# Two stacked transformer blocks in fp32 on one core: the "up" products of five feed-forward stages are turned, so that weight tiles are held in TensorE and the rows of both token tiles move

## The chip, the cores and the metric

The kernel runs on one core of one Trainium2 chip. The metric is the time of one execution in microseconds (us), as the device counts it. Engines are named as in the profile: PE is TensorE (matrix products), DVE is VectorE, ACT is ScalarE, POOL is GpSimd, SP issues most of the transfers.

## The reference, cut to what matters

256 rows (two token tiles of 128) with 1024 columns go through four layers. The first two layers each have a gated feed-forward part, a mixing part of four attention and convolution branches, and a second gated feed-forward part. The last two layers each have an attention part with gates and a plain feed-forward part.

```python
def _swiglu(x, w_in, w_out):                      # 1024 -> 2 x 2816 -> 1024
    gate, up = jnp.split(x @ w_in, 2, axis=-1)
    return (jax.nn.silu(gate) * up) @ w_out

hn = _modulate(_rms_norm(h, norm_g[l, 2]), sh3, sc3)
h = h + 0.5 * g3[:, None, :] * _swiglu(hn, ffn2_w_in[l], ffn2_w_out[l])

h = rmsnorm(x, norm_mlp)                          # 1024 -> 4096 -> 1024
return x + jnp.square(jax.nn.relu(h @ w_up)) @ w_down
```

All inputs are fp32, and so is the result.

## The kernel before, in words

**Stages.** The program is one straight list of instructions for each engine. Ten stages follow each other: 0 feed-forward, 1 mixing, 2 feed-forward, 3 feed-forward, 4 mixing, 5 feed-forward (layers one and two), then 6 attention, 7 feed-forward (called `mlp`), 8 attention, 9 `mlp` (layers three and four). A feed-forward stage has an up phase (`gemm_in`) and an out phase (`gemm_out`).

**Products in three parts.** An fp32 operand is split into `hi` (rounded to the type fp32r) and `lo`, the rest: ScalarE casts `hi`, VectorE subtracts to get `lo`. A product is then three fp32r products that add up in one PSUM bank: hi·hi, hi·lo and lo·hi. Weights come from memory in chunks of 512 KB (`fetch`, issued by SP), and `pump` converts each chunk into `hi` and `lo` on ScalarE and VectorE. `chunk()` hands them to the products in order. Tiles come from an arena of 40 buffers of 4 KB in each partition (`c` in the names of the profile).

**The up phase.** `gemm_in` goes over blocks of 512 output columns (11 in a gated part: 256 gate and 256 up columns; 8 in an `mlp`). For each block it goes over the two token tiles `tt`, and for each of these over eight slices `k` of 128 inputs. The 128x128 slice of the normed, transposed rows (`xT`) is held in the array and 512 columns of weights move:

```python
pe.matmul(ps[:, :n], xh, hi[:, k2], start=k == 0, stop=False)
pe.matmul(ps[:, :n], xh, lo[:, k2], start=False, stop=False)
pe.matmul(ps[:, :n], xl, hi[:, k2], start=False, stop=k == KT - 1)
```

The bank then holds rows by columns. `evac` reads it: in a gated part ScalarE takes the silu of the gate half, VectorE multiplies by the up half; in an `mlp` ScalarE takes the relu, scaled by the rows' norm `n_.rs[tt]`, and VectorE squares it. The result (tile `ev`, 4 buffers) is needed the other way round, with the hidden columns on partitions. So `turn`, a background task, transposes it on TensorE in pieces of 128x128 into another bank, from which ScalarE and VectorE split it into `hi` and `lo`. A gated block has two pieces for each `tt`, an `mlp` block four.

**The out phase.** `gemm_out` holds slices of the hidden rows and moves 512 columns of weights, three products each, in four banks; `residual_gated` and `residual_plain` add the result to `h`.

**What sets the order.** `Plan` keeps a modelled clock for each engine while the program is recorded. Background tasks (`bg`) are recorded between products when their modelled due time has come; `pump` converts chunks ahead while the modelled VectorE and ScalarE are not late. The order is then fixed; on the chip each engine goes through its own list and waits for semaphores. Stages 0, 2, 3 and 5 also stream modulation weights (`ada_w`) between the chunks: `ada_unit` does one VectorE instruction of 1024 columns for each (`CUSTOM_DVE_ANT_0` or `SCALAR_TENSOR_TENSOR c<-c,cond,c`). Nearly all instructions are recorded through one helper, line 183, so the profile is read by tiles and shapes.

Of the kernel before, what the change touches and what calls it, by code (L numbers as in the profile page):

```python
# [70 lines left out]
class Plan:  # L71
# [10 lines left out]
    @staticmethod  # L82
    def box(ap):

        pitch = ap.ap[0][0]
        p, a = divmod(ap.offset, pitch)
        return p, p + ap.ap[0][1], a, a + 1 + sum(s * (n - 1) for s, n in ap.ap[1:])

    @staticmethod
    def meet(a, b):  # L90
        return a[0] < b[1] and b[0] < a[1] and a[2] < b[3] and b[2] < a[3]
# [5 lines left out]
    def put(self, table, ap, stamp):  # L97

        box = self.box(ap)
        kept = [e for e in table.get(ap.name, ()) if not (box[0] <= e[0][0] and e[0][1] <= box[1] and box[2] <= e[0][2] and e[0][3] <= box[3]  # L100
                                                         and (table is self.written or e[1][1] == stamp[1]))]
        table[ap.name] = kept + [(box, stamp)]
# [140 lines left out]
def two_blocks(ctx: ExitStack, tc, w, out, dbg=None, stages=99):  # L243
# [14 lines left out]
    arena = Ring(pool, "c4", NARENA)  # L258
    evr = Ring(pool, "ev", 4)
# [337 lines left out]
    class Normed:  # L597
# [40 lines left out]
        def chain(self, tt):  # L638
# [10 lines left out]
            yield from until(lambda: room(3 if self.keep else 2))  # L649
            self.xT[tt] = arena.take([P, KT, P], R), arena.take([P, KT, P], R)  # L650
            if self.keep:
                self.x[tt] = arena.take([P, KT, P])
# [13 lines left out]
        def free(self):  # L666
            arena.put(6 if self.keep else 4)
# [123 lines left out]
    def gemm_in(n_, blocks, evac):  # L791

        whole, nb = range(4), len(blocks)
        if st["want"] == 0:
            order = [(b, tt, whole[c:c + 1]) for c in whole for b in range(EARLY) for tt in range(2)]
            order += [(b, tt, whole) for b in range(EARLY, nb) for tt in range(2)]
            mine["quota"] = 8
        else:
            order = [(b, tt, whole) for b in range(nb) for tt in range(2)]
# [4 lines left out]
        for b, tt, part in order:  # L804
            n = width(blocks[b])
            if part[0] == 0:
                wait(lambda: psr.has(1), "bank")
                acc[b, tt] = psr.take([P, 512])
                mine["held"] += 1
            ps = acc[b, tt]  # L810
            for ci in part:
# [4 lines left out]
                for k2 in range(2):  # L816
                    k = 2 * ci + k2
                    n_.finish(tt, k)
                    if lo is None:
                        pe.matmul(ps[:, :n], n_.x[tt][:, k], hi[:, k2], start=k == 0, stop=k == KT - 1)  # L820
                    else:
                        xh, xl = n_.xT[tt][0][:, k], n_.xT[tt][1][:, k]
# [989 lines left out]
```

## Time and profile before

| what | value |
|---|---|
| median of 3 runs | 1907.07 us (1906.06 to 1907.81) |
| profiled execution, its own time | 1907.24 us |
| span in its trace (first to last instruction) | 1905.5 us |
| TensorE busy, matrix products | 1864.3 us (98%) |
| TensorE weight loads (beside the products) | 1487.9 us (78%) |
| VectorE busy | 1303.6 us (68%) |
| ScalarE busy | 972.5 us (51%) |
| granted TensorE clock, mean | 0.996 |
| memory read | 394.69 MB, 208 GB/s over the span |

From the writes to `h` in the trace, the stages end near 217, 338, 527, 715, 832, 1018, 1275, 1459, 1716 and 1905 us. The up phases of the stages that the change touches are 338 to 463 (stage 2), 527 to 652 (3), 832 to 957 (5), 1275 to 1370 (7) and 1716 to 1811 (9). A busy share is an average: a busy TensorE is not one at its peak, and the spacing of its products says more.

### The profile page before, as it was taken

How to read it: one execution, taken by the hardware profiler on the slowest of the kernel's cores; microseconds unless marked ns; L12 is line 12 of the kernel's file. 1: busy time of each engine (PE TensorE's matmuls, PEld its weight loads, DVE VectorE, ACT ScalarE, POOL GpSimd, SP SyncE). 2: the span in 40 equal slices, each digit the busy share in tenths (PEclk: the TensorE clock that was granted, in tenths of full speed). 3: DMA queues.
4: the chain of work that ended last, by engine and by line, in shares of the span. 5: the costliest groups of instructions: out<-in, count | busy, mean ns of one | idle time of the engine just before them, and what ended most of it. 6: DMA issues, size and time to landing. Idle time of an engine off the chain costs nothing.

```text
span 1905.5 us, 23848 instructions
## 1 busy us (share of the span) xinstructions
PE 1864.3 (98%) x8672; PEld 1487.9 (78%) x8672; DVE 1303.6 (68%) x2044; ACT 972.5 (51%) x1506; POOL 17.0 (1%) x56
## 2 busy tenths in 40 slices
PE   6999999999999999999999999999999999999998
PEld 5788864888888886668888787888888787888886
DVE  7999796878697967865566646676654546666561
ACT  5544545444454545654445646555543645645460
POOL 0000000000000000000000000000000000000000
PEclk9999999999999999999999999999999999999999
DMA  9989752678688865435565343655574343654460
GB/s 384 382 329 394 259 192 78 234 268 297 246 296 288 334 240 194 156 130 189 192 239 188 111 155 102 215 170 167 180 250 141 125 159 107 197 195 160 146 220 34
DMA packets 110579, 397.32 MB, mean 209 GB/s; under 512 B 12278, under 2 KB 12406, under 8 KB 110460
## 3 DMA queue, kind: packets, MB, share of 16 engines
q1 hardware_dynamic: 109020, 391.88, 59.4%
q10 hardware_dynamic: 1440, 3.91, 0.6%
q8 instruction: 68, 1.11, 0.2%
q14 instruction: 51, 0.42, 0.1%
HBM read 394.69 MB, written 1.05 MB: 208 GB/s over the span
## 4 chain that ended last, share of the span: by engine, by line
PE 87%; DVE 5%; ACT 5%; issue 1%; DMA 1%; POOL 0%; ACTq 0%; POOLq 0%; DVEq 0%
PE bank L183 87%; DVE c L183 3%; ACT sm L183 2%; ACT c L183 2%; DVE sm L183 1%; ACT L175 1%; DMA cond_row<-in_c_dram 0%; DVE ev L183 0%; DMA c<-in_ada_w_dram 0%; DMA c<-in_w_out_b_dram 0%; DVE st L183 0%; DVE h L183 0%; ACT ev L183 0%; ACT junk L183 0%; ACT dl L183 0%
## 5 line engine op out<-in xcount | busy, mean ns | idle before, releaser
L183 PE MATMUL bank<-c,c 128*128 128x512 f32 (+3 forms) x7392 | 1761.9, 396 | 10.9 <-ACT c L183 7.8
L183 PEld LDWEIGHTS bank<-c,c 128*128 128x128 f32 (+1 forms) x7392 | 1350.0, 188 | 327.4 <-issue 45.8
L183 DVE TENSOR_TENSOR c<-c,c 128x1024 fp32r<-128x1024 f32 (+4 forms) x614 | 711.5, 1182 | 233.4 <-ACT c L183 225.4
L183 ACT CAST c<-c 128x1024 fp32r<-128x1024 f32 (+4 forms) x600 | 592.0, 1025 | 112.7 <-PE bank L183 74.7
L183 ACT ACTIVATE ev<-bank 128x256 f32<-128x256 f32 (+1 forms) x100 | 40.0, 401 | 198.4 <-PE bank L183 196.2
L183 DVE CUSTOM_DVE_ANT_0 c<-c,cond_row,col 128x1024 f32<-128x1024 f32 x96 | 121.9, 1275 | 0.0
L183 ACT CAST c<-bank 128x512 fp32r<-128x512 f32 (+1 forms) x100 | 55.2, 553 | 86.5 <-PE bank L183 86.5
L183 DVE TENSOR_TENSOR c<-bank,c 128x512 fp32r<-128x512 f32 (+2 forms) x108 | 69.6, 647 | 24.1 <-ACT c L183 24.1
L183 DVE TENSOR_TENSOR ev<-ev,bank 128x256 f32<-128x256 f32 x88 | 36.4, 417 | 67.4 <-ACT ev L183 67.1
L183 ACT ACTIVATE ev<-bank,st 128x512 f32<-128x512 f32 x56 | 38.5, 688 | 77.6 <-PE bank L183 77.6
L183 ACT ACTIVATE junk<-h 128x512 f32<-128x512 f32 x44 | 27.8, 631 | 95.2 <-DVE h L183 94.8
L183 PEld LDWEIGHTS bank<-con,ev 128*128 128x128 f32 x432 | 55.9, 140 | 25.5 <-issue 4.9
L183 PE MATMUL bank<-con,ev 128*128 128x128 f32 x432 | 72.3, 273 | 3.2 <-DVE ev L183 3.2
L183 ACT CAST c<-ev 128x512 fp32r<-128x512 f32 x28 | 17.4, 620 | 91.4 <-DVE ev L183 91.2
L183 ACT ACTIVATE c<-bank,st 128x512 f32<-128x512 f32 x36 | 24.8, 688 | 75.2 <-PE bank L183 69.7
L183 DVE SCALAR_TENSOR_TENSOR c<-c,cond,c 128x1024 f32<-128x1024 f32 x42 | 53.7, 1278 | 0.0
L183 DVE TENSOR_TENSOR ev<-ev 128x512 f32<-128x512 f32 x32 | 22.1, 690 | 45.5 <-ACT ev L183 45.5
L183 DVE TENSOR_TENSOR ev<-bank,c 128x512 f32<-128x512 f32 x40 | 27.4, 685 | 34.4 <-PE bank L183 34.3
L183 DVE SCALAR_TENSOR_TENSOR c<-c,col,c 128x256 f32<-128x256 f32 x120 | 48.8, 474 | 0.0
L183 ACT ACTIVATE sm<-sm,st 128x128 f32<-128x128 f32 x72 | 31.8, 443 | 17.3 <-DVE st L183 17.3
L183 DVE TENSOR_TENSOR h<-h,bank 128x512 f32<-128x512 f32 x16 | 10.9, 682 | 42.1 <-PE bank L183 42.1
L183 DVE TENSOR_TENSOR c<-ev,c 128x512 fp32r<-128x512 f32 x28 | 19.4, 692 | 23.1 <-ACT c L183 23.0
(106 smaller groups left out, 676.0 us busy)
## 6 DMA issues: line engine op xcount, KB each, us to landing
c<-in_ffn_w_in_dram SPq DMA_DIRECT2D x176, 512.0 KB, 4.8
c<-in_w_in_dram SPq DMA_DIRECT2D x152, 512.0 KB, 4.2
c<-in_ada_w_dram SPq DMA_DIRECT2D x144, 512.0 KB, 5.9
c<-in_ffn_w_out_dram SPq DMA_DIRECT2D x88, 512.0 KB, 5.5
c<-in_w_up_dram SPq DMA_DIRECT2D x64, 512.0 KB, 4.2
c<-in_w_down_dram SPq DMA_DIRECT2D x64, 512.0 KB, 4.3
c<-in_w_out_dram SPq DMA_DIRECT2D x16, 512.0 KB, 4.4
c<-in_w_o_dram SPq DMA_DIRECT2D x16, 512.0 KB, 4.2
```

What stands on the lines that cost most here:

```text
L175: self.eng.preload_act_table_set(table)
L183: return fn(*args, **kw)
```

## The change

In the up phases of stages 2, 3, 5, 7 and 9 the blocks from the third on (`b >= ALONE`, 2) are turned. A 128x128 slice of the weights is held, and the rows of both token tiles move. For this the split rows of every norm lie in one fixed tile `X` of 128 x (8 slices, 4, 128): for each slice `k` hi of tile 0, hi of tile 1, lo of tile 0, lo of tile 1. One product of weight `hi` with all four (512 columns) and one of weight `lo` with the two hi parts (256 columns) replace the three. The bank then has hidden columns on partitions: its first half collects hi·hi and lo·hi, its second half the rows' lo part, and the halves are added afterwards. Nothing has to be transposed. A block is done in two passes (`pairs[tt]`) of two banks each: in a gated part a pass has 128 gate and the 128 matching up columns.

Since tokens now lie along the columns, the `mlp` can't scale by row before the relu; the square of the norm factor (`r2`) is applied in the residual instead, for all blocks of the `mlp`. The arena goes from 40 to 36 buffers, and a norm no longer takes 4 of them. The planner's bookkeeping (`box`, `meet`, `within`) is refined to follow parts of `X`; it records no instructions.

```diff
-    NRAW, NBASE, NMOST, NARENA, SPARE = 8, 18, 16, 40, 6
+    NRAW, NBASE, NMOST, NARENA, SPARE = 8, 18, 16, 36, 6
+    ALONE = 2
+    X = pool.tile([P, KT, 4, P], R, name="X")
...
-            yield from until(lambda: room(3 if self.keep else 2))
-            self.xT[tt] = arena.take([P, KT, P], R), arena.take([P, KT, P], R)
+            self.xT[tt] = X[:, :, tt], X[:, :, 2 + tt]
...
-            order = [(b, tt, whole) for b in range(nb) for tt in range(2)]
+            order = [(b, tt, whole, bool(pairs) and b >= ALONE) for b in range(nb) for tt in range(2)]
...
-                wait(lambda: psr.has(1), "bank")
-                acc[b, tt] = psr.take([P, 512])
-                mine["held"] += 1
+                wait(lambda: psr.has(1 + both), "bank")
+                acc[b, tt] = tuple(psr.take([P, 2, S]) for _ in range(2)) if both else psr.take([P, 512])
+                mine["held"] += 1 + both
...
+                    if both:
+                        n_.finish(0, k)
+                        n_.finish(1, k)
+                        for i, j in enumerate(pairs[tt]):
+                            a = slice(P * j, P * j + P)
+                            pe.matmul(ps[i], hi[:, k2, a], X[:, k], start=k == 0, stop=False)
+                            pe.matmul(ps[i][:, 0], lo[:, k2, a], X[:, k, 0:2], start=False, stop=k == KT - 1)
...
+        def parts(b, x):
+            yield from until(lambda: hid.room(2 * b))
+            hi, lo = hid.at(2 * b)
+            a = slice(2 * (b % 2), 2 * (b % 2) + 2)
+            split(x, hi[:, a], lo[:, a])
+            evr.put()
+
+        def turned(b, g, ps):
+            wait(lambda: evr.has(2 - g), "ev")
+            if g == 0:
+                made[b] = evr.take([P, 2, S])
+            s, x = evr.take([P, S]), made[b]
+            sc_.copy(s, ps[0][:, 1])
+            sc_.copy(x[:, g], ps[1][:, 1])
+            ve.tensor_tensor(s, s, ps[0][:, 0], op=OP.add)
+            ve.tensor_tensor(x[:, g], x[:, g], ps[1][:, 0], op=OP.add)
+            sc_.activation(s, s, AF.Silu)
+            done_bank(2)
+            ve.tensor_tensor(x[:, g], x[:, g], s, op=OP.mult)
+            evr.put()
+            if g == 1:
+                hid.pend.setdefault(2 * b, []).append(bg.add(parts(b, x), urgent=True, due=plan.ready(x)))
...
-        gemm_in(n_, FFN_BLOCKS, evac)
+        gemm_in(n_, FFN_BLOCKS, evac, () if n_.first else ((0, 2), (1, 3)), turned)
...
-            sc_.activation(x, ps, AF.Relu, scale=n_.rs[tt])
+            sc_.activation(x, ps, AF.Relu)
...
+        def turned(b, g, ps):
+            wait(lambda: evr.has(1), "ev")
+            x = evr.take([P, 2, S])
+            for i in range(2):
+                sc_.copy(x[:, i], ps[i][:, 1])
+            for i in range(2):
+                ve.tensor_tensor(x[:, i], x[:, i], ps[i][:, 0], op=OP.add)
+            done_bank(2)
+            sc_.activation(x, x, AF.Relu)
+            ve.tensor_tensor(x, x, x, op=OP.mult)
+            hid.pend.setdefault(4 * b, []).append(bg.add(parts(b, g, x), urgent=True, due=plan.ready(x)))
...
+            if hf == 0:
+                ve.tensor_tensor(r2[:, tt:tt + 1], n_.rs[tt], n_.rs[tt], op=OP.mult)
+            ve.scalar_tensor_tensor(hs, ps, r2[:, tt:tt + 1], hs, op0=OP.mult, op1=OP.add)
...
-        gemm_in(n_, UP_BLOCKS, evac)
+        gemm_in(n_, UP_BLOCKS, evac, ((0, 1), (2, 3)), turned)
```

On TensorE, in the up phase of stage 5 before, two slices `k` of one token tile stand like this (the names are output bank, moving weight tile, held row tile), with two transposes of an earlier result among them:

```order
L183 MATMUL bank273_7762<-c41060_7589,c41016_7243 128x512
L183 MATMUL bank273_7762<-c41061_7590,c41016_7243 128x512
L183 MATMUL bank273_7762<-c41060_7589,c41017_7244 128x512
L183 MATMUL bank272_7719<-con_67,ev210_7759 128x128 x2
L183 MATMUL bank273_7762<-c41065_7645,c41016_7243 128x512
L183 MATMUL bank273_7762<-c41066_7646,c41016_7243 128x512
L183 MATMUL bank273_7762<-c41065_7645,c41017_7244 128x512
```

The same engine in the same phase after, two slices `k` of one pass (the names are output bank, moving `X`, held weight tile):

```order
L191 MATMUL bank300_8319<-X_63,c41054_8130 128x512
L191 MATMUL bank300_8319<-X_63,c41055_8131 128x256
L191 MATMUL bank301_8320<-X_63,c41054_8130 128x512
L191 MATMUL bank301_8320<-X_63,c41055_8131 128x256
L191 MATMUL bank300_8319<-X_63,c41057_8144 128x512
L191 MATMUL bank300_8319<-X_63,c41058_8145 128x256
```

A slice `k` of a whole block was 6 products of 512 columns; it is 4 of 512 and 4 of 256, and the transposes are gone from the turned blocks. Over the program the transposes from `ev` go from 432 to 228, and 1248 products of 256 columns are new.

On VectorE, in the up phase of stage 3 before, the work from one split into a hidden tile to the next split into it (`c<-bank,c` 128x512 is the split of the transposed bank, `c<-c,c` 128x1024 the conversion of a chunk, `SCALAR_TENSOR_TENSOR` a modulation unit):

```order
L183 TENSOR_TENSOR c4780_5344<-bank175_5264,c4779_5343 128x512
L183 TENSOR_TENSOR ev152_5354<-ev151_5353,bank176_5316 128x256
L183 TENSOR_TENSOR c4782_5377<-c4763_5226,c4781_5376 128x1024
L183 SCALAR_TENSOR_TENSOR c4758_5199<-c4766_5274,cond_72,c4758_5199 128x1024
L183 TENSOR_TENSOR c4786_5392<-c4767_5277,c4785_5391 128x1024
L183 SCALAR_TENSOR_TENSOR c4758_5199<-c4770_5289,cond_72,c4758_5199 128x1024
L183 TENSOR_TENSOR ev154_5404<-ev153_5403,bank177_5357 128x256
L183 TENSOR_TENSOR c4790_5412<-c4771_5292,c4789_5411 128x1024
L183 SCALAR_TENSOR_TENSOR c4758_5199<-c4774_5304,cond_72,c4758_5199 128x1024
L183 TENSOR_TENSOR c4780_5344<-bank178_5364,c4779_5343 128x512
```

VectorE after, at the same place, a split and the two passes of the block that follows it:

```order
L191 TENSOR_TENSOR c4764_5620<-ev137_5627,c4763_5619 128x512
L191 TENSOR_TENSOR ev141_5740<-ev141_5740,bank194_5685 128x256
L191 TENSOR_TENSOR ev140_5739<-ev140_5739,bank195_5686 128x256
L191 TENSOR_TENSOR ev140_5739<-ev140_5739,ev141_5740 128x256
L191 TENSOR_TENSOR c4778_5762<-c4759_5611,c4777_5761 128x1024
L191 SCALAR_TENSOR_TENSOR c4742_5473<-c4762_5617,cond_73,c4742_5473 128x1024
L191 TENSOR_TENSOR c4742_5473<-c4742_5473,c4743_5474 1x1024
L191 TENSOR_TENSOR c4782_5788<-c4767_5661,c4781_5787 128x1024
L191 TENSOR_TENSOR ev142_5797<-ev142_5797,bank196_5747 128x256
L191 TENSOR_TENSOR ev140_5739<-ev140_5739,bank197_5748 128x256
L191 TENSOR_TENSOR ev140_5739<-ev140_5739,ev142_5797 128x256
L191 TENSOR_TENSOR c4785_5819<-c4768_5664,c4784_5818 128x1024
```

Where one multiplication stood for each token tile, each pass now has two additions and a multiplication of 256 columns in the same list as the chunk conversions; the split of the hidden tile reads `ev` and not a bank.

## Rows read from the trace of the kernel before

**Rows 1.** The page: busy time by engine, and the chain that ended last.
```profile
PE 1864.3 (98%) x8672; PEld 1487.9 (78%) x8672; DVE 1303.6 (68%) x2044; ACT 972.5 (51%) x1506; POOL 17.0 (1%) x56
...
PE 87%; DVE 5%; ACT 5%; issue 1%; DMA 1%; POOL 0%; ACTq 0%; POOLq 0%; DVEq 0%
```

**Rows 2.** Windows, up phases of stages 2, 3, 5, 7: stretch, length, busy.
```profile
core 0: us, PE busy (x) PEld busy (x) DVE busy (x) ACT busy (x) POOL busy (x), PEclk, DMA share, GB/s
338.00:463.00 125.00, 125.00 (x573) 102.23 (x572) 96.65 (x126) 59.41 (x87) 0.74 (x2) 1.00 0.76 263
527.00:652.00 125.00, 125.00 (x573) 102.45 (x573) 105.96 (x139) 60.18 (x88) 0.74 (x2) 1.00 0.84 295
832.00:957.00 125.00, 125.00 (x574) 102.23 (x573) 75.03 (x89) 58.45 (x85) 0.74 (x2) 1.00 0.58 195
1275.00:1370.00 95.00, 95.00 (x450) 78.33 (x449) 60.00 (x66) 50.47 (x67) 0.74 (x2) 1.00 0.48 150
```

**Rows 3.** Timeline of PE, up phase of stage 5: start, length, group.
```profile
870.00 0.38 PE L183 MATMUL bank<-con,ev 128*128 128x128 f32 x2
870.14 5.74 PE L183 MATMUL bank<-c,c 128*128 128x512 f32 x24
...
955.67 0.38 PE L183 MATMUL bank<-con,ev 128*128 128x128 f32 x2
```

**Rows 4.** Timeline of PE, up phase of stage 7.
```profile
1323.15 0.60 PE L183 MATMUL bank<-con,ev 128*128 128x128 f32 x4
1323.50 5.74 PE L183 MATMUL bank<-c,c 128*128 128x512 f32 x24
...
1358.75 0.60 PE L183 MATMUL bank<-con,ev 128*128 128x128 f32 x4
```

**Rows 5.** Tile bank on PE, out phase of stage 7 (1380 to 1440): first and last start.
```profile
L183 PE MATMUL bank<-c,c x266: 389/389/389, 1379.7 to 1439.8; 128*128 128x512 f32 x133
```

**Rows 6.** Groups by form, PE, 231 to 235: products of 260 columns (stage 1).
```profile
L183 PE MATMUL bank<-c,c 128*128 128x260 f32 x24 | 3.0, 281 | 0.0
```

**Rows 7.** Groups by form, weight loads (PEld), 231 to 235 and 1380 to 1440.
```profile
L183 PEld LDWEIGHTS bank<-c,c 128*128 128x128 f32 x29 | 3.9, 188 | 0.2
...
L183 PEld LDWEIGHTS bank<-c,c 128*128 128x128 f32 x265 | 49.7, 188 | 10.3
```

**Rows 8.** Groups by form, DVE, 527 to 652 (up phase of stage 3).
```profile
L183 DVE TENSOR_TENSOR c<-c,c 128x1024 fp32r<-128x1024 f32 x44 | 53.2, 1218 | 5.3 <-ACT c L183 4.8 <-DMA c<-in_ada_w_dram 0.5
L183 DVE CUSTOM_DVE_ANT_0 c<-c,cond_row,col 128x1024 f32<-128x1024 f32 x22 | 28.1, 1276 | 0.0
L183 DVE SCALAR_TENSOR_TENSOR c<-c,cond,c 128x1024 f32<-128x1024 f32 x7 | 8.9, 1278 | 0.0
L183 DVE TENSOR_TENSOR ev<-ev,bank 128x256 f32<-128x256 f32 x21 | 8.7, 416 | 10.4 <-ACT ev L183 10.4
L183 DVE TENSOR_TENSOR c<-bank,c 128x512 fp32r<-128x512 f32 x10 | 6.8, 684 | 0.7 <-ACT c L183 0.7
L183 DVE TENSOR_TENSOR c<-ev,c 128x512 fp32r<-128x512 f32 x2 | 1.4, 687 | 0.7 <-ACT c L183 0.7
```

**Rows 9.** Groups by form, DVE, 338 to 463 (up phase of stage 2).
```profile
L183 DVE TENSOR_TENSOR c<-c,c 128x1024 fp32r<-128x1024 f32 x41 | 49.7, 1221 | 7.5 <-ACT c L183 6.9 <-DMA c<-in_ffn_w_in_dram 0.5
...
L183 DVE TENSOR_TENSOR ev<-ev,bank 128x256 f32<-128x256 f32 x22 | 9.2, 418 | 16.3 <-ACT ev L183 16.3
```

**Rows 10.** Groups by form, ACT, 527 to 652.
```profile
L183 ACT ACTIVATE ev<-bank 128x256 f32<-128x256 f32 x22 | 8.4, 383 | 47.2 <-PE bank L183 47.2
L183 ACT CAST c<-bank 128x512 fp32r<-128x512 f32 x10 | 5.9, 587 | 13.4 <-PE bank L183 13.4
...
L183 ACT CAST c<-ev 128x512 fp32r<-128x512 f32 x2 | 1.2, 620 | 2.3 <-DVE ev L183 2.3
```

**Rows 11.** Groups by form, DVE, then ACT, 1275 to 1370 (up phase of stage 7).
```profile
L183 DVE TENSOR_TENSOR ev<-ev 128x512 f32<-128x512 f32 x16 | 11.0, 690 | 22.8 <-ACT ev L183 22.8
L183 DVE TENSOR_TENSOR c<-bank,c 128x512 fp32r<-128x512 f32 x15 | 10.4, 690 | 3.5 <-ACT c L183 3.5
...
L183 ACT ACTIVATE ev<-bank,st 128x512 f32<-128x512 f32 x16 | 11.0, 690 | 29.2 <-PE bank L183 29.2
```

More of the change, by code (lines that the diff above doesn't have):

```diff
@@ L99, in put @@
         box = self.box(ap)
-        kept = [e for e in table.get(ap.name, ()) if not (box[0] <= e[0][0] and e[0][1] <= box[1] and box[2] <= e[0][2] and e[0][3] <= box[3]
-                                                         and (table is self.written or e[1][1] == stamp[1]))]
+        kept = [e for e in table.get(ap.name, ()) if not (self.within(e[0], box) and (table is self.written or e[1][1] == stamp[1]))]
         table[ap.name] = kept + [(box, stamp)]
@@ L666, in free @@
         def free(self):
-            arena.put(6 if self.keep else 4)
+            arena.put(2 if self.keep else 0)
     class Final(Normed):
@@ L788, in rows_ready, with gemm_in @@
             upcoming.pop(0)
-    def gemm_in(n_, blocks, evac):
+    def gemm_in(n_, blocks, evac, pairs=(), turned=None):
         whole, nb = range(4), len(blocks)
         if st["want"] == 0:
-            order = [(b, tt, whole[c:c + 1]) for c in whole for b in range(EARLY) for tt in range(2)]
-            order += [(b, tt, whole) for b in range(EARLY, nb) for tt in range(2)]
+            order = [(b, tt, whole[c:c + 1], False) for c in whole for b in range(EARLY) for tt in range(2)]
+            order += [(b, tt, whole, False) for b in range(EARLY, nb) for tt in range(2)]
             mine["quota"] = 8
         else:
-            order = [(b, tt, whole) for b in range(nb) for tt in range(2)]
+            order = [(b, tt, whole, bool(pairs) and b >= ALONE) for b in range(nb) for tt in range(2)]
             if not n_.there[1] or n_.there[1][-1] < KT:
@@ L803, in gemm_in @@
         held, acc = {}, {}
-        for b, tt, part in order:
+        for b, tt, part, both in order:
             n = width(blocks[b])
             if part[0] == 0:
-                wait(lambda: psr.has(1), "bank")
-                acc[b, tt] = psr.take([P, 512])
-                mine["held"] += 1
+                wait(lambda: psr.has(1 + both), "bank")
+                acc[b, tt] = tuple(psr.take([P, 2, S]) for _ in range(2)) if both else psr.take([P, 512])
+                mine["held"] += 1 + both
             ps = acc[b, tt]
@@ L831, in gemm_in, with done_bank @@
             if part[-1] == 3:
[L832 to L833 removed]
+                drain([n_.e[0], n_.e[1]] if both else [n_.e[tt]])
+                (turned if both else evac)(b, tt, acc.pop((b, tt)))
                 mine["quota"] = 3
[L836 to L838 removed]
+    def done_bank(n=1):
+        psr.put(n)
+        mine["held"] -= n
     def gemm_out(nk, lhs, evac, skew, used=lambda k: None):
```

46 lines of the change are left out of this document (31 added, 15 removed).

## The prediction

> **What bounds the kernel now.** I read the busy times first, then the chain, then the stretches that change. TensorE is busy for 98% of the span and makes up 87% of the chain that ended last [rows 1]. In the up phases of stages 2, 3, 5 and 7, TensorE is busy without a break, at a granted clock of 1.00 [rows 2]; stage 9 repeats stage 7. So there time is saved only if TensorE has less to do, and lost if another engine can't keep up. The nearest is VectorE: 105.96 of 125 us in stage 3, 96.65 in stage 2, but 75.03 in stage 5 and 60.00 of 95 in stage 7.
>
> What a product costs is read from where it starts. In an out phase 266 products of 512 columns start from 1379.7 to 1439.8: 60.1 / 265 = 0.2268 us each [rows 5], so 24 take 5.44. In an up phase the same 24 come with a run of transposes. In stage 5 fifteen such periods go from 870.00 to 955.67: 85.67 / 15 = 5.711 us [rows 3]. A run of two transposes thus costs 5.711 - 5.443 = 0.268 us. In stage 7 six periods go from 1323.15 to 1358.75: 5.933 us, so a run of four costs 0.490 us [rows 4].
>
> **What goes.** Three gated stages have 9 turned blocks each, 27 in all, two `mlp` stages 6 each, 12 in all; a block has two runs.
> Gated: 27 x 2 x 0.268 = 14.5 us less. `mlp`: 12 x 2 x 0.490 = 11.8 us less. These are 108 + 96 = 204 transposes, the difference of 432 and 228.
>
> **What the products cost.** The columns that move are the same: 6 x 512 = 4 x (512 + 256). But there are eight products where six were. No row has 256 columns of this type. The nearest has 260: 24 products in 3.0 us, the last of which is shown with its whole length of 0.281, so (3.0 - 0.281) / 23 = 0.118 us each [rows 6]. Half of a 512-column product would be 0.113. I take 0.118, since 260 is next to 256, and keep 0.113 as the lower end. A slice `k` then takes 4 x 0.2268 + 4 x 0.118 = 1.379 us for 1.361 before: 0.0184 more, and over 8 slices and 39 blocks 5.7 us more (0 at the lower end).
>
> Each product loads its own weights, and a load is recorded with 188 ns [rows 7], more than the 118 of a short product. In rows 6 and 7, loads of 188 ns stand beside products that start every 0.118 us, so a load does not hold up the next product for its length. The Trainium skill, "TensorE: Matmul & The Clock Gate", says in Part 3 (The mechanism) that a weight load overlaps products in flight only when it goes to another row group; in Part 2 it also allows a load into a background buffer. By the first sentence alone, full-height loads as here would be paid, and the sum would be that of the third rival below; the trace agrees with the second, and with it the sum stays as worked out.
>
> **What VectorE and ScalarE get.** For a gated block VectorE loses two multiplications of 256 columns (0.416) and the split from a bank (0.684), 1.52 us, and gets four additions and two multiplications of 256 and the split from `ev` (0.687), 6 x 0.416 + 0.69 = 3.18 us [rows 8]: 1.67 more, 15.0 us over 9 blocks. TensorE's time for the same stretch becomes 125 - 18 x 0.268 + 9 x 8 x 0.0184 = 121.5 us. VectorE then needs 105.96 + 15.0 = 121.0 us in stage 3 and 111.7 in stage 2, but 90 in stage 5. For an `mlp` block it loses 2 x 0.69 + 2 x 0.69 = 2.76 [rows 11] and gets 4 x 0.416 + 4 x 0.69 = 4.42: 10 us more over 6 blocks, 70 of about 90. ScalarE loses two reads of 0.383 and a split of 0.587 in a gated block and gets six of about 0.383 and one of 0.62 [rows 10]: 1.57 more, 74 of 121.5 us in stage 3. In an `mlp` block it loses 2 x 0.690 [rows 11] and two splits, and gets four copies, two relus and two splits: about 1.5 more, 59 of 90. So only stages 2 and 3 can turn over.
>
> There VectorE also waits inside its own list. In stage 3 it stood idle for 125 - 106 = 19 us, 10.4 of it at `ev<-ev,bank` and 4.8 at conversions, for ScalarE [rows 8]; in stage 2 16.3 and 6.9 [rows 9]. Much of the first is waiting for TensorE to end a block, which a late VectorE doesn't pay. What stays is a pass's round trip: after the second addition the multiplication waits for the silu, and the next conversion for a cast behind that silu. If all 16 us stayed, stage 3 would need 137 us of VectorE against 121.5, 15.6 too many, and stage 2 111.7 + 23.9 = 135.6, 14.1 too many. Behind such a delay stand, in VectorE's list, the converted chunks that TensorE wants next. In the order of the changed kernel, 1 to 4 chunks of later blocks stand ahead of the first bank read of a block in stage 3, and the second pass of the block at hand needs no new one: a cover of 5.5 + (1 to 4) x 2.76, or 8 to 16 us. Half of the waits kept (8 us) are covered in both stages; all of them leave 15.6 - 8 + 14.1 - 8 = 14 us. I take 3 us, nearer to the covered end, and keep 0 and 14.
>
> **The rest.** `residual` of an `mlp` becomes a `SCALAR_TENSOR_TENSOR`; at 1024 columns that form takes 1278 ns for 1218 [rows 8], so below 0.1 us, and with the small square of the norm about 0.2 us at the end of stage 9; at stage 7 TensorE's next products cover it. Stage 0, the mixing and the attention stages keep their products. The arena has 36 buffers where 40 less 4 were used in up phases: the same; in out phases it is four fewer, which only shortens how far chunks are converted ahead; I cost it at nothing, and without chunks ahead TensorE would wait there for `c<-c,c`.
>
> **The sum.** Against the profiled execution's own time of 1907.24 us (its span of 1905.5 and 1.74 around it; the median is 1907.07, so the same): 1907.24 - 14.5 - 11.8 + 5.7 + 3 + 0.2 = 1889.8, say 1890 us.
>
> **Rivals.**
> *VectorE becomes the bound in stages 2 and 3.* For it: 121.0 of 121.5 us in stage 3, before any wait. Against it: the chunks ahead, and a lighter out phase behind each. It gives the sum without the 3, plus 7 to 14 us: 1894 to 1901. The Trainium skill calls VectorE and ScalarE strict first-in-first-out queues ("TensorE: Matmul & The Clock Gate", table at the top); the waits of rows 8 and 9, with work queued behind them, agree.
> *A part of the transposes' time is not theirs.* In rows 3 and 4 the first product starts 0.14 and 0.35 us after the run's start; the rest of the 0.268 and 0.490 shows as slower products behind it, which might come from the change of banks and stay. Then 54 x 0.14 + 24 x 0.35 = 16.0 us go, not 26.3: 1900. Against it: in the out phase the banks change at each product and 24 take 5.44.
> *Weight loads come through (slower).* Place: each 256-column product, behind which a load of 188 ns must fit into 118. If alternating lengths break the overlap that a run of 260-column products shows, 70 ns are added 4 x 8 x 39 = 1248 times: 87 us, about 1977 us. It makes the kernel slower from 14 ns a product on (17.4 / 1248). Against it: rows 6 and 7, where the loads are the same and even closer.
> *Nothing changes* would need some 20 of the 30 us by which VectorE falls short in rival one to come through, with a cover of a third; the order gives more cover than that.
>
> **How the numbers follow.** A measurement of this kernel can tell about 0.2%, or 3.8 us, from no change. Forecast (products as worked out, waits up to 6 us): 0.64, 1883 to 1894. VectorE bound: 0.20, 1894 to 1901, its tail beyond 1903 included. Part of the transposes stays: 0.08, about 1900. Loads come through, in part or whole: 0.05. Others: 0.03. The range takes in the lower end of the products (1884), a little below it for waits that vanish with the transposes, and rivals one and two: 1879 to 1903. Faster by over 0.2% are the forecast, rival two and nearly all of rival one: 0.89. Slower: 0.06, the loads and a part of the others. The same: 0.05.
>
> **What would show it.** Right: PE in the up phases of stages 5 and 7 starts a pair of 512 and 256 columns every 0.345 us without transposes; a pass of 32 products takes 5.52 us, a stage 5 up phase 3.5 us less, stage 7 and 9 about 5 us less each. VectorE in 527 to 650 near 97% busy with TensorE idle for a few us at most. Wrong: PE idle for conversions (`c<-c,c` by DVE or ACT) for over 10 us in stages 2 and 3; a spacing of pairs near 0.41 us (loads); slower first products in each pass (bank changes). A VectorE that runs later than its order assumes is the likeliest way to be wrong.

## The result, and the profile after

The changed kernel takes 1917.57 us (median of four runs, 1916.88 to 1917.99); the kernel before took 1907.44 us beside it (four runs). The ratio is 1.0054, with an interval of 1.0037 to 1.0071: 10 us slower, where 17 us faster was forecast. The profiled execution has a span of 1915.1 us for 1905.5. Runs of one kernel lie up to 4.5 us apart with their mean granted clock: those of the kernel before, beside all experiments, go from 1903.5 us at 0.999 to 1908.0 at 0.994.

The page, busy times and the chain that ended last, answers to [rows 1]:

```profile
PE 1868.5 (98%) x9092; PEld 1503.6 (79%) x9092; DVE 1359.4 (71%) x2202; ACT 1025.9 (54%) x1664; POOL 17.0 (1%) x56
...
PE 75%; issue 11%; DVE 7%; ACT 5%; DMA 1%; POOL 0%; POOLq 0%; ACTq 0%; DVEq 0%
```

TensorE is busy for 4.2 us more, though 204 transposes of it are gone, and the chain holds less of TensorE and more of "issue" and VectorE. Up phases of stages 2, 3, 5 and 7 in windows, as in [rows 2]:

```profile
core 0: us, PE busy (x) PEld busy (x) DVE busy (x) ACT busy (x) POOL busy (x), PEclk, DMA share, GB/s
338.00:460.00 122.00, 121.04 (x664) 103.70 (x663) 105.54 (x155) 69.67 (x119) 0.74 (x2) 1.00 0.74 258
528.00:650.00 122.00, 117.00 (x623) 98.97 (x623) 107.69 (x155) 66.22 (x111) 0.74 (x2) 0.99 0.78 272
845.00:965.00 120.00, 120.00 (x665) 103.46 (x664) 87.52 (x122) 67.96 (x115) 0.00 (x0) 1.00 0.59 195
1290.00:1380.00 90.00, 90.00 (x489) 77.21 (x488) 65.31 (x87) 56.30 (x89) 0.74 (x2) 1.00 0.46 150
```

Stages 5 and 7 run without a break, as before. In stage 3 TensorE stands for 5 of 122 us, in stage 2 for 1; before it stood for none.

The turned products of stage 5: first those of both lengths together (count, shortest, median and longest record, first and last start), then by form (count, busy, mean length of a record).

```profile
L191 PE MATMUL bank<-X,c x341: 279/391/399, 899.8 to 959.8; 128*128 128x512 f32 x171
```

```profile
L191 PE MATMUL bank<-X,c 128*128 128x512 f32 x171 | 60.5, 396 | 0.0
L191 PE MATMUL bank<-X,c 128*128 128x256 f32 x170 | 48.0, 282 | 0.0
```

From 899.8 to 959.8 there are 340 steps, 170 pairs: 60.0 / 170 = 0.353 us for a pair of 512 and 256 columns. The prediction had 0.345. In an out phase, by the same view, nothing changed from [rows 5]: (1439.9 - 1383.7) / 248 = 0.2266.

```profile
L191 PE MATMUL bank<-c,c x249: 388/389/390, 1383.7 to 1439.9; 128*128 128x512 f32 x125
```

But in stage 6, which isn't turned, the products that hold a slice of `X` got slower. The kernel before, then the changed one, where 36 products of another phase stand among them:

```profile
L183 PE MATMUL bank<-c,c x143: 389/389/389, 1198.7 to 1230.9; 128*128 128x512 f32 x143
```

```profile
L191 PE MATMUL bank<-c,X x104: 392/396/399, 1201.6 to 1233.9; 128*128 128x512 f32 x104
L191 PE MATMUL bank<-c,c x36: 388/389/398, 1222.2 to 1230.1; 128*128 128x512 f32 x36
```

Before, 142 steps take 32.2 us, 0.2268 each. After, 139 steps take 32.3 us; with 0.2268 for each of the 36, the others take (32.3 - 8.2) / 103 = 0.234 us. The ends of such a stretch are read to 0.1 us, so a quotient like this is good to 0.001.

Stage 3 has two kinds of stalls. Timeline of TensorE at its start (start, length, group, idle time before it and what ended that):

```profile
529.14 0.50 PE L191 MATMUL bank<-c,X 128*128 128x512 f32 x1 [0.99 <-ACT c L191]
531.23 1.20 PE L191 MATMUL bank<-c,X 128*128 128x512 f32 x2 [1.59 <-DVE c L191]
...
540.67 0.73 PE L191 MATMUL bank<-c,X 128*128 128x512 f32 x2 [0.76 <-DVE c L191]
```

and late in its up phase:

```profile
637.09 1.44 PE L191 MATMUL bank<-X,c 128*128 128x256 f32 x7 [0.56 <-DVE c L191]
638.81 0.50 PE L191 MATMUL bank<-X,c 128*128 128x512 f32 x1 [0.28 <-ACT c L191]
640.07 5.68 PE L191 MATMUL bank<-X,c 128*128 128x256 f32 x31 [0.76 <-DVE c L191]
...
653.66 6.55 PE L191 MATMUL bank<-X,c 128*128 128x256 f32 x36 [0.77 <-DVE c L191]
```

All the waits are for `c`, the conversions of weights by ScalarE and VectorE. Windows show the clock behind the first of them, in the changed kernel and then in e1, an experiment below with stalls of 1.10 and 1.59 us at the same place (the 0.66 and the 1.00 ahead of the DMA share are the granted clock):

```profile
531.00:536.00 5.00, 4.77 (x18) 4.08 (x19) 4.07 (x5) 3.06 (x6) 0.00 (x0) 0.66 0.48 148
```

```profile
531.00:536.00 5.00, 4.66 (x25) 3.94 (x26) 4.95 (x8) 3.17 (x7) 0.00 (x0) 1.00 0.54 186
```

Behind two stalls of 0.99 and 1.59 us, part of the next 5 us ran at the lower of the clock's two levels. In e1 it did not, although TensorE was busy for the same 2.65 of the 5 us from 526 to 531 in both. So the fall can come on top of such stalls and need not.

VectorE in the up phase of stage 3, by form, for [rows 8]:

```profile
L191 DVE TENSOR_TENSOR c<-c,c 128x1024 fp32r<-128x1024 f32 x41 | 49.5, 1221 | 7.9 <-ACT c L191 7.9
...
L191 DVE TENSOR_TENSOR ev<-ev,bank 128x256 f32<-128x256 f32 x34 | 12.8, 413 | 0.4 <-ACT ev L191 0.4
...
L191 DVE TENSOR_TENSOR ev<-ev,ev 128x256 f32<-128x256 f32 x15 | 6.4, 426 | 2.3 <-ACT ev L191 2.3
```

It no longer waits for ScalarE at the banks (0.4 us for 10.4). But it waits 7.9 us at the conversions where it waited 4.8, and 2.3 us at the new multiplication behind the silu. It does 41 conversions in 122 us where it did 44 in 125. At the end of an `mlp`, the new form of `residual` takes 750 ns in the median, that of the attention stages 680: 70 ns more for each of eight.

### The profile page after: what moved, and what is told of

It is laid out like the page before. It is cut to its first block, busy times and chain, and to the rows that moved or that the text cites. A ratio compares the mean times of both kernels' runs of the same rounds, so it can differ in the third digit from the quotient of the medians.

```text
span 1915.1 us, 24999 instructions
## 1 busy us (share of the span) xinstructions
PE 1868.5 (98%) x9092; PEld 1503.6 (79%) x9092; DVE 1359.4 (71%) x2202; ACT 1025.9 (54%) x1664; POOL 17.0 (1%) x56
## 3 DMA queue, kind: packets, MB, share of 16 engines
q10 hardware_dynamic: 1440, 3.91, 0.6%
## 4 chain that ended last, share of the span: by engine, by line
PE 75%; issue 11%; DVE 7%; ACT 5%; DMA 1%; POOL 0%; POOLq 0%; ACTq 0%; DVEq 0%
PE bank L191 75%; DVE c L191 4%; ACT c L191 2%; DVE sm L191 2%; ACT sm L191 1%; ACT L183 1%; DVE ev L191 1%; DVE st L191 0%; ACT ev L191 0%; ACT X L191 0%; DMA cond_row<-in_c_dram 0%; DVE h L191 0%; DVE X L191 0%; DMA ws<-in_gmlp_ws_dram 0%; POOL st L191 0%
## 5 line engine op out<-in xcount | busy, mean ns | idle before, releaser
L191 DVE TENSOR_TENSOR c<-c,c 128x1024 fp32r<-128x1024 f32 x596 | 704.0, 1203 | 232.0 <-ACT c L191 225.4
L191 PE MATMUL bank<-c,X 128*128 128x512 f32 (+1 forms) x2832 | 690.0, 398 | 17.3 <-ACT c L191 9.3
L191 PE MATMUL bank<-c,c 128*128 128x512 f32 (+4 forms) x2688 | 648.2, 401 | 0.0
L191 ACT CAST c<-c 128x1024 fp32r<-128x1024 f32 x582 | 584.3, 1039 | 114.3 <-PE bank L191 90.0
L191 PEld LDWEIGHTS bank<-c,X 128*128 128x128 f32 x2832 | 519.9, 189 | 144.1 <-ACT c L191 12.3
L191 PEld LDWEIGHTS bank<-c,c 128*128 128x128 f32 (+2 forms) x2688 | 484.9, 188 | 130.4 <-issue 40.4
L191 PE MATMUL bank<-X,c 128*128 128x512 f32 x2496 | 445.0, 339 | 3.4 <-DVE c L191 3.0
L191 PEld LDWEIGHTS bank<-X,c 128*128 128x128 f32 x2496 | 384.2, 188 | 62.4 <-DVE c L191 4.9
L191 ACT COPY ev<-bank 128x256 f32<-128x256 f32 x156 | 55.3, 373 | 110.1 <-PE bank L191 109.7
L191 ACT ACTIVATE ev<-ev 128x256 f32<-128x256 f32 (+1 forms) x78 | 37.8, 484 | 86.1 <-DVE ev L191 84.6
L191 ACT CAST X<-ev 128x512 fp32r<-128x512 f32 x28 | 17.4, 621 | 89.7 <-DVE ev L191 89.5
```

Of the source, the lines that this page charges most:

```text
L191: return fn(*args, **kw)
```

## The experiments

Each experiment is compared with runs of the kernel before taken beside it; a ratio is to these, with its 95% interval in brackets. Stage times are worked out from the ends of VectorE's last addition to `h` in each stage. In us:

| kernel | stage 0 | 3 | 4 | 5 | 6 | span |
|---|---|---|---|---|---|---|
| before | 217.5 | 187.4 | 118.0 | 186.0 | 257.0 | 1905.5 |
| changed | 220.8 | 197.5 | 118.1 | 185.1 | 260.7 | 1915.1 |
| e1, X on the arena's grid | 219.6 | 196.4 | 118.4 | 185.0 | 257.1 | 1906.7 |
| e7, e1 not turned | 219.3 | 194.6 | 118.4 | 186.1 | 257.1 | 1911.4 |
| e6, e1 with SPARE 2 | 217.9 | 191.8 | 128.0 | 184.9 | 261.0 | 1915.6 |
| e11, X in the arena | 218.4 | 192.5 | 117.3 | 184.9 | 256.9 | 1897.0 |
| e12, stage 3 held | 217.9 | 187.4 | 115.7 | 184.9 | 256.9 | 1892.4 |

### Where X lies: e1, e2, e3, e4

In the built program the arena's buffers lie at 2624 modulo 4096 bytes of a partition, and `X` at 1152. e1 only asks for `X` later, just ahead of the arena, so that it lies at 2624 too.

```diff
-    X = pool.tile([P, KT, 4, P], R, name="X")
+    X_ = []
+    def place():
+        if not X_:
+            X_.append(pool.tile([P, KT, 4, P], R, name="X"))
+        return X_[0]
...
+                place()
                 rows = arena.take([P, D])
...
+            X = place()
             self.xT[tt] = X[:, :, tt], X[:, :, 2 + tt]
```

> The changed kernel with X placed directly ahead of the arena, so that X and the arena's buffers have the same address modulo 4096 (2624), as every operand of these products had before; nothing else moves. Placement theory (products whose two operands lie differently in SBUF run slower): the products with X go from 0.2335 back to 0.2268 us, 3984 of 512 columns x 6.7 ns = 26 us less, so about 1891 us. Rival, the turned form itself or VectorE's load is the cause: no change, 1917 us. Rival, one big tile X with a stride of 2 KB between slices is slower to read: no change, 1917.

Measured: 1906.63 us, ratio 0.9999 (0.9990 to 1.0009), 0.55% or 10.5 us better than the changed kernel. Stage 6 of e1, then its turned pairs:

```profile
L191 PE MATMUL bank<-c,X x107: 389/389/389, 1198.7 to 1230.9; 128*128 128x512 f32 x107
L191 PE MATMUL bank<-c,c x36: 389/389/389, 1218.6 to 1226.6; 128*128 128x512 f32 x36
```

```profile
L191 PE MATMUL bank<-X,c x341: 277/395/403, 899.8 to 959.8; 128*128 128x512 f32 x171
```

32.2 us for 142 steps are 0.2268 each: the products with held slices of `X` are as fast as in the kernel before, and stage 6 takes 257.1 us for 260.7. The turned pairs stay at 0.353, and stage 3 at 196.4: these two have other causes. `X` is still one tile with the same stride, so the second rival is out. Of the 26 us expected 10.5 came. 1248 of the 3984 products counted are turned and didn't move; why the other 2736 gave back 10.5 us and not 18 was not followed up.

e2 keeps `X` where the change put it and turns no block.

```diff
-        gemm_in(n_, FFN_BLOCKS, evac, () if n_.first else ((0, 2), (1, 3)), turned)
+        gemm_in(n_, FFN_BLOCKS, evac)
-        gemm_in(n_, UP_BLOCKS, evac, ((0, 1), (2, 3)), turned)
+        gemm_in(n_, UP_BLOCKS, evac)
```

> The changed kernel with X and the smaller arena, but no block turned: all products and transposes as before. Placement theory: 4608 products with X slower by 6.7 ns, less those that already ran slower behind transposes, so 15 to 30 us over before, 1922 to 1937 us, and stage 3 begins without a stall. Rival, the turned form or VectorE's added load costs the time: 1907 us as before. If the arena of 36 buffers is what stalls the start of stage 3, that stall (about 5 us) is here too.

Measured: 1931.08 us, ratio 1.0138 (1.0123 to 1.0153). Stage 6:

```profile
L191 PE MATMUL bank<-c,X x95: 392/398/398, 1214.8 to 1244.9; 128*128 128x512 f32 x95
L191 PE MATMUL bank<-c,c x36: 388/389/397, 1227.8 to 1235.8; 128*128 128x512 f32 x36
```

The products that hold `X` take (30.1 - 8.2) / 94 = 0.233 us, and now there are more of them. e7 (below) is e2 with `X` on the grid: 1.0038. So the place alone is worth 1.0% when no block is turned. Stage 3 takes 196.7 us in e2, with TensorE waiting 2.6 us at its start: that stall, too, is there without a turned block.

e3 moves all arena buffers of the kernel before by 64 bytes, e4 leaves 64 bytes between `X`'s place and the grid.

```diff
 e3, ahead of the arena's first buffer
+                if not shift:
+                    shift.append(pool.tile([P, 16], F, name="shift"))
...
 e4, in place()
+            pool.tile([P, 16], F, name="sa")
+            X_.append(pool.tile([P, KT, 4, P], R, name="X"))
+            pool.tile([P, 16], F, name="sb")
```

> The kernel before with all arena buffers moved by 64 bytes, both operands of the products together. If only the distance of the two operands counts: products stay at 0.2268 us, 1907 us. If the address of an operand itself counts (64 modulo 128 good, 0 modulo 128 bad): up to 6912 products x 6.7 ns = 46 us more, 1953 us.

> The changed kernel with X ahead of the arena, but 64 bytes off the arena's address modulo 4096 (2688 and 2752). If any distance that is no multiple of 128 costs: products with X at 0.2335, 1917 us. If only larger distances cost: 0.2268, about 1891 us.

Measured, one run each: 1905.88 and 1910.51 us. The out phase of e3, then stage 6 of e4:

```profile
L183 PE MATMUL bank<-c,c x266: 389/389/389, 1379.8 to 1439.9; 128*128 128x512 f32 x133
```

```profile
L191 PE MATMUL bank<-c,X x106: 388/392/394, 1198.8 to 1231.0; 128*128 128x512 f32 x106
L191 PE MATMUL bank<-c,c x36: 388/389/389, 1219.6 to 1227.5; 128*128 128x512 f32 x36
```

In e3 a product takes 60.1 / 265 = 0.2268: where both operands lie in itself doesn't matter. In e4 the products of `X` take (32.2 - 8.2) / 105 = 0.2286. The step from 0.2268 is small against the reading of the ends, but the median record grows with it, 392 ns for 389. Thus it is the distance between the two operands' places that counts where a slice of `X` is held: 0.2268 us at none, 0.2286 at 64 bytes, 0.234 where the change put it. Where `X` moves, in the turned pairs, 0.353 stood at either place. Three distances give no rule, and none is claimed.

### The pair: e5, e8, e9

e5 is e1 with the products of a turned pass in groups, per chunk four of 512 columns and then four of 256:

```diff
+for k2 in range(2):
+    k = 2 * ci + k2
+    for i, j in enumerate(pairs[tt]):
+        pe.matmul(ps[i], hi[:, k2, P * j:P * j + P], X[:, k], start=k == 0, stop=False)
...
+for k2 in range(2):
+    k = 2 * ci + k2
+    for i, j in enumerate(pairs[tt]):
+        pe.matmul(ps[i][:, 0], lo[:, k2, P * j:P * j + P], X[:, k, 0:2], start=False, stop=k == KT - 1)
```

> This is e1 (the changed kernel with X laid where the arena's buffers lie) with one change: in a turned pass the four products of 512 columns of a chunk come first and the four of 256 columns behind them, where they alternated. In e1 a turned pair takes 353.6 ns from start to start, 236 to the next of the 512 and 117 of the 256; the prediction had 345. Theory, that the alternation of lengths costs the difference: six of eight transitions now join equal lengths, 512 to 512 at 227 ns and 256 to 256 at 113 to 118 ns, a pair takes about 346 ns, and 1248 pairs give back 8 to 11 us: 1896 to 1899 us against 1906.6 of e1. Rival, that a product of 512 columns costs 236 whenever X moves, or with weights of a 128-column slice: a pair stays at 352 to 354 ns in whatever order, and the time stays at 1905 to 1908 us.

Measured: 1905.69 us, ratio 1.0003 (0.9994 to 1.0013).

```profile
L191 PE MATMUL bank<-X,c x345: 278/389/398, 899.6 to 959.8; 128*128 128x512 f32 x87, 128*128 128x256 f32 x86
```

A pair takes 60.2 / 172 = 0.350: between the two expectations. In the trace the products of 512 still start 232 ns apart in the mean, and those of 256 118. The time does not show the 3 ns gained for each pair: TensorE's late waits in stage 3 grew from 2.6 us in e1 to 4.6. So neither theory stood, and e8 and e9 were made for what was left. e8 gives every turned product 512 columns:

```diff
-pe.matmul(ps[i][:, 0], lo[:, k2, a], X[:, k, 0:2], start=False, stop=k == KT - 1)
+pe.matmul(ps[i], lo[:, k2, a], X[:, k], start=False, stop=k == KT - 1)
```

> This is e1 with every product of a turned pass 512 columns wide: the low halves of the weights also take all 512 columns of X (the term of low by low, which the reference's precision doesn't ask for, is computed as well), so that lengths never change within a pass. The time is not the point (1248 products grow by some 109 ns, 136 us more). Theory, that a change of length disturbs the products of 512 behind it, as the transposes do in the kernel before: the products stand at 226 to 227 ns from start to start through the pass. Rival, that products with X as the moving operand and a 128-column slice as weights are slower as such: they alternate between 230 and 236, 232 to 233 in the mean, as in e5 within its groups of four.

```profile
L191 PE MATMUL bank<-X,c x266: 388/389/390, 924.7 to 984.8; 128*128 128x512 f32 x133
```

60.1 us for 265 steps, 0.2268 each, the same count in the same time as in [rows 5] (the kernel as a whole takes 2025.83 us, as it does more work). Moving `X` past a 128-column slice of weights is thus no slower; changing the length is.

e9 puts the sixteen products of 512 columns of a pass ahead of its sixteen of 256.

```diff
+for cj in part:
...
+            pe.matmul(ps[i], cs[cj][0][:, k2, P * j:P * j + P], X[:, k], start=k == 0, stop=False)
...
+for cj in part:
...
+            pe.matmul(ps[i][:, 0], cs[cj][1][:, k2, P * j:P * j + P], X[:, k, 0:2], start=False, stop=k == KT - 1)
```

> This is e1 with the sixteen products of 512 columns of a turned pass first and its sixteen of 256 columns behind them. Theory, that about ten products behind a change of length are disturbed and the rest are not, as behind the transposes of the kernel before: the first ten of a group of sixteen alternate between 230 and 236 ns, the last six start every 227, and the mean is 229 to 231. Rival, that these products are slower as such: all sixteen alternate, mean 232 to 233, as in e5. The time is then 1903 to 1906 us either way, too close to tell the two.

Measured, one run: 1902.78 us. Groups by form over the first microsecond of the products of 512 in a pass (903.2 to 904.2), and over the last eleven (904.6 to 906.8):

```profile
L191 PE MATMUL bank<-X,c 128*128 128x512 f32 x5 | 1.3, 394 | 0.0
...
L191 PE MATMUL bank<-X,c 128*128 128x512 f32 x11 | 2.7, 389 | 0.0
```

The first five records have 394 ns in the mean, the last eleven 389. By their starts the first five of this pass stand 234, 235, 229, 232 and 231 ns apart, the others 226 or 227. The disturbance is real and dies out, but behind five products, not ten.

The kernel before had shown the same behind a run of two transposes. Groups by form behind the run at 870.00 of [rows 3] (870.2 to 872.6), then for the rest of that period (872.7 to 875.6):

```profile
L183 PE MATMUL bank<-c,c 128*128 128x512 f32 x11 | 2.8, 401 | 0.0
...
L183 PE MATMUL bank<-c,c 128*128 128x512 f32 x14 | 3.3, 389 | 0.0
```

### The stalls: e6, e7

e6 is e1 with `SPARE` at 2 for 6, so that the planner converts as many chunks ahead as it did with four buffers more.

```diff
-    NRAW, NBASE, NMOST, NARENA, SPARE = 8, 18, 16, 36, 6
+    NRAW, NBASE, NMOST, NARENA, SPARE = 8, 18, 16, 36, 2
```

> This is e1 with the planner's SPARE, the buffers that it leaves free when it converts a chunk ahead, at 2 where it was 6, which makes up in the out phases for an arena of 36 where 40 were. The order then has 1, 1, 4, 5, 5 converted chunks ahead of the last bank reads of stage 2, as in the kernel before (e1 has 0, 0, 2, 3, 3). Theory, that the four missing buffers made the stalls at the starts of stages 3 and 2: stage 3 takes 188 to 190 us where e1 took 196, and the time falls to 1898 to 1900 us. Rival, that VectorE's added work in the turned blocks made them: the stalls stay, at least those late in the stage (635 to 655 us), stage 3 takes 194 us or more, and the time stays above 1904 us.

Measured: 1917.66 us, ratio 1.0062 (1.0045 to 1.0079). Timeline of TensorE at the start of stage 3, and late in it:

```profile
526.00 1.03 PE L191 MATMUL bank<-con,c 128*128 128x128 f32 x8
526.79 1.62 PE L191 MATMUL bank<-c,X 128*128 128x512 f32 x6
```

```profile
615.61 0.50 PE L191 MATMUL bank<-X,c 128*128 128x512 f32 x1 [0.34 <-ACT c L191]
616.87 9.98 PE L191 MATMUL bank<-X,c 128*128 128x256 f32 x56 [0.76 <-DVE c L191]
627.56 1.44 PE L191 MATMUL bank<-X,c 128*128 128x256 f32 x7 [0.71 <-DVE c L191]
...
644.12 6.27 PE L191 MATMUL bank<-X,c 128*128 128x256 f32 x34 [0.76 <-DVE c L191]
```

There is no idle time at the start, but all of the late ones are there: each theory holds for one kind of stall. Stage 3 falls from 196.4 to 191.8 us. The kernel as a whole gets slower, for it loses more elsewhere: stage 4 goes from 118.4 to 128.0 us, stage 6 from 257.1 to 261.0. Between 720 and 840 TensorE waits 8.8 us for 5.2 in e1, and the granted clock of stage 4 is 0.95 for 0.99. That these stages miss the buffers which `SPARE` kept free for them is likely, but no run tested it.

e7 is e1 with the two lines of e2, no block turned, so that the smaller arena is left alone.

> This is the changed kernel with X laid where the arena's buffers lie and no block turned (rows held and weights moving everywhere, as in the kernel before): what is left of the change is the arena of 36 buffers and X beside it. Theory, that four fewer buffers cost time by themselves: stage 3 takes 195 us or more with TensorE waiting for conversions at its start, stages 5, 7 and 9 take as long as in the kernel before (186, 184, 189), and the time is 1912 to 1918 us. Rival, that the buffers cost nothing, as I had taken, and the stalls belong to the turned blocks: stage 3 takes 187 to 188 us and the time is that of the kernel before, 1905 to 1908 us.

Measured: 1913.14 us, ratio 1.0038 (1.0023 to 1.0053), 7.1 us above the kernel before (4.4 to 10.1 by the interval). Its timeline at the start of stage 3 and late in it:

```profile
527.09 0.50 PE L191 MATMUL bank<-c,X 128*128 128x512 f32 x1 [1.10 <-ACT c L191]
529.19 1.22 PE L191 MATMUL bank<-c,X 128*128 128x512 f32 x2 [1.59 <-DVE c L191]
...
621.63 5.74 PE L191 MATMUL bank<-c,X 128*128 128x512 f32 x24
627.21 0.38 PE L191 MATMUL bank<-con,ev 128*128 128x128 f32 x2
627.35 8.46 PE L191 MATMUL bank<-c,X 128*128 128x512 f32 x36
```

The stalls at the start are there without a single turned block; the late ones are not. So the first come with the smaller arena, and the late ones with the turned blocks.

e1 against e7 is the turning by itself, on the grid and with the small arena in both: 1906.63 us for 1913.14, by the ratios 0.39% or 7.4 us faster.

### A version without the losses: e11, e12, e13

e11 is e5 (products in groups) with `X` in four buffers of the arena, two slices `k` in each, taken for a turned stage and given back behind its up phase; the arena has 40 buffers again.

```diff
+if self.both:
+    yield from until(lambda: self.X is not None or room(4))
+    if self.X is None:
+        self.X = [arena.take([P, 2, 4, P], R, tag="X") for _ in range(KT // 2)]
```

> This is e5 with X taken apart into four buffers of the arena (two slices k each), taken when a stage's norm begins and given back behind its up phase; the arena has 40 buffers again, and the token rows are split in quarters instead of halves. At the last bank reads of stage 2, 1, 1, 4, 5, 5 converted chunks stand ahead, as in the kernel before. Theory, that the four lasting buffers cost the 7 us that e7 measured: the stall at the start of stage 3 (near 526 us) is gone, those of VectorE near 615 to 645 stay, and the time is 1897 to 1900 us, faster than the kernel before by 0.3 to 0.5%. Rival, that the stall comes with the turned blocks ahead of it: it stays, and the time is 1903 to 1906 us.

Measured: 1899.07 us, ratio 0.9962 (0.9949 to 0.9974). No wait is left between 520 and 545. TensorE's waits between 600 and 660 (sum, count, longest):

```profile
PE bank L191 <- ACT c L191: 3.4, 3, 1.8
PE bank L191 <- DVE c L191: 0.6, 1, 0.6
```

The late waits are put down to ScalarE here, but ScalarE had itself waited for VectorE. TensorE, then ScalarE, at the longer of the two waits for ScalarE before 640:

```profile
631.46 9.02 PE L191 MATMUL bank<-X,c 128*128 128x512 f32 x48 [0.97 <-ACT c L191]
```

```profile
630.05 0.42 ACT L191 ACTIVATE ev<-ev 128x256 f32<-128x256 f32 x1 [3.72 <-DVE ev L191]
630.38 3.88 ACT L191 CAST c<-c 128x1024 fp32r<-128x1024 f32 x4
```

The casts that TensorE wants stand in ScalarE's list behind a silu, and the silu waited 3.72 us for VectorE's addition. From 600 to 640 VectorE goes from one instruction to the next and waits only for ScalarE: 0.15 us behind a silu, 0.51 us behind a cast.

e12 leaves stage 3, the fourth norm of the list, as it was before the change.

```diff
...
-first=not norms, both=bool(norms) and i != 1))
+first=not norms, both=bool(norms) and i != 1 and len(norms) != 3))
...
```

> This is e11 with stage 3 not turned. In stage 3 turning takes away 18 runs of transposes (4.8 us) and adds 9 x 32 pairs at some 350 ns for 340 (2.9 us), so that 1.9 us of gain go with it. Theory, that VectorE's added work in stage 3 makes the stalls of 4 to 5 us near 615 to 645 us that e6 still had and e7 had not: they are gone, stage 3 takes 187 to 188 us, and the time is 2 to 3 us below that of e11, 1894 to 1898 us. Rival, that the stalls come from elsewhere (the stream of loads, the arena): they stay, and the time is 1 to 2 us above that of e11.

Measured: 1894.00 us, ratio 0.9933 (0.9920 to 0.9947); the late stalls are gone, stage 3 is back at 187.4 us, and the step is 5.1 us where 2 to 3 were expected. Timeline of TensorE late in stage 3:

```profile
622.03 8.46 PE L191 MATMUL bank<-c,c 128*128 128x512 f32 x36
630.32 0.38 PE L191 MATMUL bank<-con,ev 128*128 128x128 f32 x2
630.46 3.71 PE L191 MATMUL bank<-c,c 128*128 128x512 f32 x15
```

e13 is e12 with the order of e9, and that one's lines.

> This is e12 with the order of e9: the sixteen products of 512 columns of a turned pass first, its sixteen of 256 behind them. Theory, that five or so products behind each change of length are disturbed: a pass of 32 products, 16 x 228.5 to 229.2 and 16 x 119.6, takes 5.57 us where e12's groups of four took 16 x 231.3 + 16 x 118.8, 5.60 us; over the 60 passes that are still turned that is 2 us, and the time is 1891 to 1893 us where e12 had 1894.0. Rival, that holding a block's four chunks through the pass delays the conversions behind them: TensorE waits for them in stages 2 or 5, and the time is 1894 us or more.

Measured: 1892.71 us, ratio 0.9928 (0.9915 to 0.9942), 1.3 us below e12, where the theory had 2. The intervals of the two ratios overlap almost wholly, so this step is not shown. e12 and e13 are faster than the kernel before and than the changed one.

## Why the prediction was wrong, point by point

The forecast was 17.4 us less than before; measured were 10.1 us more. Three steps failed: the pairs of 512 and 256 columns were added up from rows of one length each (10.2 us more), the stages that keep their products were taken to keep their price (10.5 us), and the smaller arena was put at nothing (7.1 us).

**The transposes.** The 26.3 us are borne out where nothing else changes, from e7 to e1. In stage 5 the prediction's 18 runs give 4.8 us less, and pairs at 0.353 cost 9 x 8 x (4 x 0.353 - 1.361) = 3.7 us more: 1.1 less is due, and 186.1 became 185.0 us. In an `mlp` stage 12 x 0.490 - 6 x 8 x 0.051 = 3.4 less is due; stage 7 went from 181.8 to 178.4 us, stage 9 from 184.0 to 180.6. That a part of the transposes' time would stay as slower products (rival two) is refuted by e8, in which the banks change at each turned product and they start every 0.2268 us. The slower products that this rival had seen in rows 3 and 4 were real; they stand behind a change of length, and the rows by themselves could have warned of the next point.

**The products, a term of the right sign that was mis-sized.** "I take 0.118" was near for products among their like (0.118 in e5's groups of four, 0.120 in e9's of sixteen), and 0.2268 was right for 512; but they don't add up in alternation. A pair takes 0.353 for 0.345, and the term is 39 x 8 x (4 x 0.353 - 1.361) = 15.9 us, not 5.7. The third rival had looked at this place, for another reason and with a price of 70 ns; 8 ns came, less than the 14 from which it alone would decide. The loads of weights stay hidden: in e9 the 256-column products start every 120 ns, each with its own load, which agrees with the Trainium skill's background buffer ("TensorE: Matmul & The Clock Gate", Part 2) and not with its sentence on row groups (Part 3).

**"Stage 0, the mixing and the attention stages keep their products."** They kept their number, not their price. `X` as a tile of its own came to lie off the arena's grid, and a product with a held slice of it took 0.234 us. By e1 that costs 10.5 us. This step failed too, and no rival held it: I had looked at what the instructions are, not at where their operands lie.

**The arena, "I cost it at nothing".** This step failed, 7.1 us by e7. The clause behind it named the mechanism, and it came: with 36 buffers the order has 0, 0, 2, 3, 3 converted chunks ahead at the last bank reads of stage 2, where it had 1, 1, 4, 5, 5. So TensorE waits for `c<-c,c` at the start of stage 3, and with the chunks restored the wait is gone (e6, e11). In the changed kernel and in e7 the granted clock fell behind the wait (0.66 from 531 to 536; 0.78 from 526 to 531), in e1 it did not.

**VectorE in stages 2 and 3.** The 3 us that I took were about right: in e1 TensorE's late waits are 2.6 us in stage 3, and it waits 0.9 us in stage 2; in e7 it has neither. The mechanism was right too, and it is that of rival one. Of the waits for ScalarE only those at the banks nearly vanished; the round trip that the prediction described stayed, with 2.3 us at the multiplication and 7.9 us at the conversions. With its 107.69 us of work (88% of 122, and not the 97 I had named) and these waits, 118.3 of 122 us, VectorE had little left, and the conversions came late. What was wrong is how far the price carries: with the arena whole and the products in groups, turning stage 3 costs 5.1 us on balance (e11 against e12), where by its terms it should have gained 2. TensorE's waits there are 4.0 us; where the rest goes was not traced.

**The sum.** -26.3 + 15.9 + 10.5 + 7.1 + 3 = +10.2 us; measured were +10.1. The terms come from different experiments, two of them with an interval of some 3 us to either side, so the agreement to 0.1 is luck. The profiles show as much: stage 1, which no term is meant for, went from 121.1 us at a granted clock of 0.97 to 117.6 at 1.00. Open stays why the distance of two operands and a change of length matter, and which distances do.

## What to carry to other kernels

A new tile changes more than its own work: it takes buffers from whatever runs ahead, and it moves operands in memory; both are to be priced, by what is converted ahead at the moment of the highest load, and by laying the tile where the old operands lay. Add up products from a row in which lengths follow each other as they will in the new loop, and order them so that lengths change rarely. Where an engine has no slack left in one stage, leave the change out there: e12, with one stage fewer turned, is 5.1 us faster than e11.

## What the runs showed of the hardware

- With a slice of `X` held, the time from start to start of products of 512 columns depends on the distance between the places of held and moving operand: 0.2268 us at none modulo 4096 bytes, 0.2286 at 64, 0.234 at 1472 (e1, e4, the changed kernel); shifting both together changes nothing (e3, one run; e4 is one run as well). With `X` moving, in alternating pairs, no difference was seen (0.353 us in the changed kernel and in e1).
- Behind products of 256 columns the next five of 512 start 229 to 235 ns apart before they settle at 226 to 227 (e9); with one length alone all do (e8). In strict alternation that made 8 ns for each pair. Behind two transposes of 128 columns the records of the next eleven have 401 ns in the mean, those after them 389 (the kernel before).
- Behind the stalls of 0.99 and 1.59 us at the start of stage 3 the granted clock was 0.66 from 531 to 536, part of it at 1.2 GHz where 2.4 is full: 5 x 0.34 = 1.7 us of lost work on top of the stalls. Stalls of 1.10 and 1.59 us at the same place left it at 1.00 in e1. What decides between the two is open.
- Weight loads recorded with 188 ns (rows 7) did not hold up products of 256 columns for their length: these start every 120 ns (e9).
